# Softmax over 32,768 columns on one core: the first four stores in the load queue's order

## The chip, the core and the metric

The kernel runs on one core of one Trainium2 chip. The metric is device time in microseconds (us) of one execution, inputs and outputs in the chip's memory (HBM). The core's parts that matter here are VectorE (DVE), ScalarE (ACT), SyncE (SP), and the 16 DMA engines that carry data between HBM and on-chip memory (SBUF). A DMA is started by an instruction on SP or on ACT; each of the two has its own DMA queue, and the same 16 DMA engines serve both. In the profile SP's queue is q1 and ACT's is q10.

## The reference

A softmax with a temperature over the last axis of a 16 x 256 x 32768 array of float32:

```python
def reference(logits, temperature):            # temperature = 1.0
    scaled = logits / temperature
    scaled = scaled - scaled.max(axis=-1, keepdims=True)
    exp_scaled = np.exp(scaled)
    return (exp_scaled / exp_scaled.sum(axis=-1, keepdims=True)).astype(np.float32)
```

The input has 537 MB and so has the output; every byte is read once and written once.

## The kernel before

**Tiles.** The 4,096 rows are cut into halves, which gives 8,192 half rows of 16,384 elements. 128 of them, one for each SBUF partition, make a tile of 8.39 MB; there are 64 tiles, 0 to 63. A row's two halves lie on neighbouring partitions of one tile. SBUF holds three tiles at a time (`_BUFS = 3`); tile g lives in slot g mod 3, and its result is written over its input there.

**One tile's work** (class `Work`). The tile is cut into three column pieces of 6304, 5376 and 4704 (`_PLAIN`, line 11). DVE finds the negated maximum of each piece (line 188), ACT replaces each piece by its exponential with its own maximum and sums it (line 248), DVE swaps the two half rows' maxima and sums between partitions (206), takes the row's maximum (210), ACT makes the correction factors (259), and DVE forms the factor of each piece (217 to 233). Then the pieces are scaled: the first by ACT (267), the other two by DVE (239). The last two tiles use six smaller pieces (`_LATE`).

**Loads and stores.** `load(g)` (lines 119 to 131) is issued by SP. From tile 3 on it waits until the store of tile g - 3, which had the slot before, has landed. Load 3 is cut into two halves; each half waits for the matching half of store 0 only. `store(p, engine, ...)` (lines 133 to 146) waits until the pieces that it covers are scaled, and is then issued on the engine that it is given. Store 0 has two halves, store 61 four pieces, store 63 three.

**Who issues what, in which order.** An engine's instructions run in the order in which they are written, and a waiting instruction holds up all behind it on that engine. SP's program is: all loads 0 to 63 (lines 269 and 270), then the stores of tiles 62 and 63 (271 and 272), then a wait for everything (277 and 278). ACT's program is: tiles 0 to 3 written out, each followed by its store (289 to 291), a loop of 19 turns with three tiles and their stores in each (292 to 297), and tiles 61 to 63 written out, with the store of tile 61 (298 to 301). DVE's program has the same three parts and issues no DMA. The lines that set the order of the DMAs around the change are these:

```python
    for g in range(G):
        load(g)
    for g in range(G - _TAIL + 1, G):
        store(Place(g, G), nc.sync, None)
...
    for g in range(_HEAD):
        Work(Place(g, G)).scalar()
        store(Place(g, G), nc.scalar, None)
```

Here `G` is 64, `_HEAD` 4 and `_TAIL` 3. Text and code below name a load of tile g as Lg and a store as Sg, with a and b for halves.

Of the kernel before, what the change touches and what calls it, by code (L numbers as in the profile page):

```python
# [15 lines left out]
_TAIL = 3  # L16
# [48 lines left out]
def load_parts(g):  # L65
    if g == 3:
        return [(0, _W // 2), (_W // 2, _W // 2)]
    return [(0, _W)]


def store_parts(g, n):
    if g == 0:
        return [(0, _W // 2), (_W // 2, _W // 2)]
    if g == n - _TAIL:
        return list(_NEXT_STORES)
    return list(_LAST_STORES) if g == n - 1 else [(0, _W)]


def stored(g, n):
    first = [(("st", 0, g % _BUFS), 16 * (g // _BUFS + 1))]  # L80
    return first + [(("st", i, "of", g), 16) for i in range(1, n)]
# [3 lines left out]
def kernel(  # L85
# [6 lines left out]
    nc = tc.nc  # L92
# [12 lines left out]
    G = N * 2 // P  # L105
# [13 lines left out]
    def load(g):  # L119
        p = Place(g, G)  # L120
        rows = slice(g * P, (g + 1) * P)
        for j, (s, n) in enumerate(load_parts(g)):
            if g >= _BUFS:
                parts = store_parts(g - _BUFS, G)
                tokens = stored(g - _BUFS, len(parts))
                for (a, m), (which, value) in zip(parts, tokens):
                    if a < s + n and s < a + m:
                        nc.sync.wait_ge(sig[which], value)
            where = slice(p.slot * _W + s, p.slot * _W + s + n)
            key = ("ld", j, *p.key)  # L130
            sig.dma(key, nc.sync.dma_start(out=X[:, where], in_=x[rows, s : s + n]))

    def store(p, engine, first, some=slice(None)):
        g = p.g
        rows = slice(g * P, (g + 1) * P) if first is None else bass.ds(first, P)
        for i, (s, n) in list(enumerate(store_parts(g, G)))[some]:
            if p.looped:
                engine.wait_ge(sig[("scaled", *p.key)], p.n2)
            else:
                for group in (p.own, p.on_act):  # L140
                    for k in [k for k in group if k in p.over(s, n)][-1:]:
                        engine.wait_ge(sig[("scaled", k, *p.key)], p.n)
            where = slice(p.slot * _W + s, p.slot * _W + s + n)
            sig.dma(
                stored(g, len(store_parts(g, G)))[i][0], engine.dma_start(out=o[rows, s : s + n], in_=X[:, where])  # L145
            )
# [119 lines left out]
                xs = self.piece(k)  # L266
                self.scaled(a.mul(out=xs, in_=xs, mul=f[:, k : k + 1]), k, self.p.on_act)  # L267

    for g in range(G):
        load(g)  # L270
    for g in range(G - _TAIL + 1, G):
        store(Place(g, G), nc.sync, None)
    counts = {}
    for g in range(G):
        for which, value in stored(g, len(store_parts(g, G))):
# [12 lines left out]

    for g in range(_HEAD):
        Work(Place(g, G)).scalar()  # L290
        store(Place(g, G), nc.scalar, None)
    with nc.scalar.Fori(1, 1 + turns) as turn:
        turn2 = nc.scalar.snap(turn * 2)
        for j in range(_BUFS):
# [2 lines left out]
            store(p, nc.scalar, turn * (_BUFS * P) + (_HEAD + j - _BUFS) * P)  # L297
    for g in range(G - _TAIL, G):
        Work(Place(g, G)).scalar()
        if g == G - _TAIL:  # L300
            store(Place(g, G), nc.scalar, None)


# [33 lines left out]
```

## Time and profile before

| what | value |
|---|---|
| median of 3 runs (lowest to highest) | 2485.12 us (2484.16 to 2495.25) |
| profiled execution: its own time | 2484.74 us |
| profiled execution: span of its instructions | 2483.0 us |
| VectorE busy | 1526.2 us, 61% of the span |
| ScalarE busy | 1325.5 us, 53% |
| q1 (SP's DMA queue) | 553.65 MB, 51.6% of the 16 engines' time |
| q10 (ACT's DMA queue) | 520.10 MB, 48.4% |
| read from HBM and written to it | 536.87 MB each, 432 GB/s over the span |
| loads: issue to landing, shortest, median, longest | 22.0, 43.5, 64.4 us |

The span is what the profile's pages divide into; the execution's own time has 1.7 us more around it. The two queues' shares of the DMA engines' time add up to 100%. A DMA's time from issue to landing holds its waiting in the queue and the sharing of the DMA engines with the other queue, and so grows with what is in flight beside it.

### The profile page before, as it was taken

The numbers are of one execution on the slowest core, as the hardware profiler recorded it, in microseconds if no ns is written. First come the engines' busy times: TensorE is split into PE (matmuls) and PEld (weight loads), VectorE is DVE, ScalarE is ACT, GpSimd is POOL, SyncE is SP. The second block draws the span as 40 slices with busy tenths as digits, with TensorE's granted clock in tenths as the row PEclk, the third lists the DMA queues.
The fourth block names the chain that finished last, engine by engine and source line by source line (L and its number), as shares of the span: only waits on it lengthen the run. The fifth ranks groups of instructions, "written<-read, shape, count | busy, mean of one in ns | idle before, by whom it ended". The sixth has DMA issues, their size and how long they took to land.

```text
span 2483.0 us, 1810 instructions
## 1 busy us (share of the span) xinstructions
DVE 1526.2 (61%) x776; ACT 1325.5 (53%) x529; POOL 0.2 (0%) x4
## 2 busy tenths in 40 slices
DVE  5755665656656666566665665656656566565665
ACT  4644645546455464554654646546455464554655
POOL 0000000000000000000000000000000000000000
DMA  9999999999999999999999999999999999999999
GB/s 421 420 436 423 439 438 430 433 438 435 428 439 437 425 438 437 434 430 438 436 427 438 438 431 432 438 435 428 439 436 425 439 438 434 429 439 436 425 441 394
DMA packets 19443, 1073.78 MB, mean 432 GB/s; under 512 B 2160, under 2 KB 2160, under 8 KB 2160
## 3 DMA queue, kind: packets, MB, share of 16 engines
q1 hardware_dynamic: 9936, 553.65, 51.6%
q10 hardware_dynamic: 9504, 520.10, 48.4%
q14 instruction: 3, 0.02, 0.0%
HBM read 536.87 MB, written 536.87 MB: 432 GB/s over the span
## 4 chain that ended last, share of the span: by engine, by line
DMA 71%; DVE 22%; ACT 5%; issue 0%; ACTq 0%; DVEq 0%; SPq 0%
DMA xs<-in_logits_dram 36%; DMA out_dram<-xs 35%; DVE t L188 16%; DVE xs L239 5%; ACT xs L248 5%; ACT ee L259 0%; DVE junk L233 0%; DVE t L206 0%; DVE row L230 0%; DVE row L210 0%; DVE junk L217 0%; ACTq L145 0%; DVE row L217 0%; DVEq L204 0%; SPq L332 0%
## 5 line engine op out<-in xcount | busy, mean ns | idle before, releaser
L248 ACT ACTIVATE xs<-xs,t 128x6304 f32<-128x6304 f32 (+5 forms) x198 | 932.0, 4707 | 1052.2 <-DVE t L188 1045.3
L188 DVE TENSOR_REDUCE t<-xs 128x1 f32<-128x6304 f32 (+5 forms) x198 | 1110.1, 5663 | 616.9 <-DMA xs<-in_logits_dram 616.9
L267 ACT ACTIVATE xs<-xs,junk 128x6304 f32<-128x6304 f32 (+1 forms) x68 | 355.6, 5235 | 45.0 <-DVE junk L233 45.0
L239 DVE TENSOR_SCALAR xs<-xs,junk 128x5376 f32<-128x5376 f32 (+2 forms) x130 | 358.8, 2803 | 2.3
L206 DVE LOAD_MASK_SELECT t<-t x64 | 0.9, 14 | 282.8 <-ACT xs L248 282.8
L259 ACT ACTIVATE ee<-t,row 128x6 f32<-128x6 f32 (+1 forms) x64 | 19.2, 300 | 35.2 <-DVE row L210 35.2
L248 ACT ACTIVATION_READ_ACCUMULATOR xs<-xs,t 128x1 f32 x198 | 36.9, 186 | 0.0
L217 DVE CUSTOM_DVE_ANT_1 junk<-ee,t 128x6 f32<-128x6 f32 (+1 forms) x64 | 10.7, 167 | 23.5 <-ACT ee L259 23.5
L233 DVE TENSOR_SCALAR junk<-ee,row 128x3 f32<-128x3 f32 (+1 forms) x64 | 14.6, 229 | 2.3
L230 DVE RECIPROCAL row<-row 128x1 f32<-128x1 f32 x64 | 10.5, 163 | 2.2
L210 DVE TENSOR_REDUCE row<-t 128x1 f32<-128x6 f32 (+1 forms) x64 | 10.2, 159 | 2.2
L206 DVE STREAM_SHUFFLE t<-t 128x6 f32<-128x6 f32 (+1 forms) x64 | 10.4, 163 | 0.5
L217 DVE DVE_READ_ACCUMULATOR2_ANT row<- 128x1 f32 x64 | 5.3, 83 | 0.0
L248 ACT ACT_TABLE_LOAD x1 | 1.3, 1283 | 0.9 <-SPq L111 0.9
L318 POOL MEMSET const-bfloat16-1.0<- 128x1 bf16 x1 | 0.1, 102 | 0.0
L318 POOL MEMSET const-uint8-127<- 128x1 uint8 x1 | 0.1, 102 | 0.0
L318 POOL MEMSET const-float32-1.0<- 128x1 f32 x1 | 0.1, 99 | 0.0
L318 POOL MEMSET const-float32-0.0<- 128x1 f32 x1 | 0.1, 98 | 0.2 <-issue 0.2
## 6 DMA issues: line engine op xcount, KB each, us to landing
out_dram<-xs ACTq DMA_DIRECT2D x2, 4096.0 KB, 28.4
xs<-in_logits_dram SPq DMA_DIRECT2D x2, 4096.0 KB, 35.9
out_dram<-xs ACTq DMA_DIRECT2D x4, 2048.0 KB, 41.7
out_dram<-xs SPq DMA_DIRECT2D x2, 3072.0 KB, 18.7
out_dram<-xs SPq DMA_DIRECT2D x1, 2048.0 KB, 11.5
xs<-in_logits_dram SPq DMA_DIRECT2D x63, 43.5
out_dram<-xs ACTq DMA_DIRECT2D x60, 43.4
out_dram<-xs SPq DMA_DIRECT2D x1, 27.9
```

Of the source, the lines that this page charges most:

```text
L188: m = v.tensor_reduce(out=t[:, k : k + 1], in_=self.piece(k), axis=mybir.AxisListType.X, op=A.max, negate=True,)
L206: v.stream_shuffle(out=t[:, 2 * K : 4 * K], in_=t[:, 0 : 2 * K], mask=swap), "sh"
L210: v.tensor_reduce(out=r[:, 0:1], in_=tv[:, :, 0, :], axis=mybir.AxisListType.XY, op=A.min),
L217: v.tensor_tensor_reduce(out=f[:, 0 : 2 * K].rearrange("p (a k) -> p a k", a=2), in0=self.ev, in1=tv[:, :, 1, :], scale=1.0, scalar=0.0, o ...
L230: self.done(v.reciprocal(out=r[:, 2:3], in_=r[:, 1:2]), "rc")
L233: v.tensor_scalar_mul(out=f[:, 0:K], in0=e[:, 0:K], scalar1=r[:, 2:3]), "f"
L239: v.tensor_scalar_mul(out=xs, in0=xs, scalar1=f[:, k : k + 1]), k, self.p.own
L248: s = a.activation(out=xs, in_=xs, func=Exp, bias=t[:, k : k + 1], scale=inv_t, accum_out=t[:, K + k : K + k + 1],)
L259: a.activation(out=self.ev, in_=self.tv[:, :, 0, :], func=Exp, bias=r[:, 0:1], scale=-1.0),
L267: self.scaled(a.mul(out=xs, in_=xs, mul=f[:, k : k + 1]), k, self.p.on_act)
L318: nc = _bacc.Bacc("TRN2", target_bir_lowering=False, num_devices=1)
```

## The change

SP's program becomes one list, `order(n)`, in which the stores of tiles 0 to 3 stand between loads 0 to 4. ACT no longer issues a store that is in that list: it issues none behind tiles 0 to 3, the 57 of its loop (tiles 4 to 60) as before, and that of tile 61 as before. The stores of tiles 62 and 63 stay on SP behind the last load. All waits of each load and store stay the same, and so do their sizes.

```diff
+def order(n):
+    plan = [("L", 0), ("L", 1), ("L", 2), ("S", 0), ("L", 3), ("S", 1), ("S", 2)]
+    plan += [("L", 4), ("S", 3)] + [("L", g) for g in range(5, n)]
+    return plan + [("S", n - 2), ("S", n - 1)]
...
-    for g in range(G):
-        load(g)
-    for g in range(G - _TAIL + 1, G):
-        store(Place(g, G), nc.sync, None)
+    for what, g in order(G):
+        if what == "L":
+            load(g)
+        else:
+            store(Place(g, G), nc.sync, None)
...
     for g in range(_HEAD):
         Work(Place(g, G)).scalar()
-        store(Place(g, G), nc.scalar, None)
+        if ("S", g) not in order(G):
+            store(Place(g, G), nc.scalar, None)
...
     for g in range(G - _TAIL, G):
         Work(Place(g, G)).scalar()
-        if g == G - _TAIL:
+        if ("S", g) not in order(G):
             store(Place(g, G), nc.scalar, None)
```

With its halves, SP's list begins L0, L1, L2, S0a, S0b, L3a, L3b, S1, S2, L4, S3, L5, L6 and so on.

## The prediction

> **What bounds the kernel now.** I read the page's engine shares first: DVE is busy 61% of the span and ACT 53%, so neither is the bound over the whole. Next the page's lines on DMA:
>
> ```profile
> DMA  9999999999999999999999999999999999999999
> HBM read 536.87 MB, written 536.87 MB: 432 GB/s over the span
> ```
>
> The DMA engines are busy in every one of 40 slices. The question is then how far the DMA rate falls below its best, and where; the view by stretches, at edges that I chose by the phases of the pipeline, tells (columns: stretch, length, DVE, ACT, POOL busy, PE clock, DMA share, GB/s):
>
> ```profile
> 0.00:52.00 52.00, 24.11 (x13) 21.95 (x9) 0.20 (x4) 1.00 0.99 423
> 52.00:140.00 88.00, 62.57 (x27) 49.95 (x19) 0.00 (x0) 1.00 1.00 424
> 140.00:232.00 92.00, 56.10 (x34) 53.37 (x22) 0.00 (x0) 1.00 1.01 431
> 232.00:348.00 116.00, 71.02 (x36) 61.55 (x24) 0.00 (x0) 1.00 1.00 434
> 464.00:2322.00 1858.00, 1144.99 (x577) 992.54 (x385) 0.00 (x0) 1.00 1.00 434
> 2404.00:2483.00 79.00, 48.37 (x32) 43.05 (x32) 0.00 (x0) 1.00 0.95 409
> ```
>
> From 232 us on the rate is 434 GB/s, turn after turn, with no gap. 1073.74 MB at 434 GB/s take 2474.1 us; the span is 2483.0. All that any reordering could win is the difference of 8.9 us (0.36%), and only part of it lies where this change works.
>
> Last, the chain of waits in order of time (columns: start, length, what) shows the loop's rhythm:
>
> ```profile
> 580.75 43.45 DMA out_dram<-xs
> 624.22 43.47 DMA xs<-in_logits_dram
> 667.72 17.35 DVE t L188 x3
> ...
> 690.96 5.61 DVE xs L239 x2
> 696.73 43.33 DMA out_dram<-xs
> ```
>
> A slot's round is store 43.5, load 43.5, compute and issue 29.0, together 696.73 - 580.75 = 115.98 us for three tiles in three slots, 38.66 a tile. The two transfers of one tile at 434 GB/s need 2 x 8.389 MB / 434 = 38.66 us. So the chain looks as if it alternated between load, compute and store, but its period is just the DMA engines' work. One transfer that shares the engines half and half takes 38.7 us; each takes 4.8 us more, because it queues behind its forerunner. These 2 x 4.8 = 9.6 us in each round are slack: a slot may come late by that much before an engine runs dry. "DMA-bound" is therefore what has to be tested: **does the new order ever leave the DMA engines without work, or make them slower?**
>
> **The change part by part.** The comparison of the two programs by engine shows the five DMAs of stores 0 to 3 gone from ACT and standing in SP's list where the diff puts them; nothing else moves. Five issues at 0.34 us (the duration of the store issues on ACT in the timeline) leave ACT, which sits idle 1052.2 us before line 248 waiting for DVE: worth nothing. They add five issues of 0.33 to 0.42 us to SP, which does nothing but wait and issue: cost nothing as long as the queue has work, which I now check. What ACT's waits for scaling held up was only ACT's own next exponential, and that waits for DVE's maximum anyway.
>
> Units: one tile is 19.3 us of the 16 engines (8.389 MB / 434 GB/s). The first loads confirm it with a single queue at work: by the issue view of narrow windows, L0 is issued at 0.94 and lands 22.0 later (22.9), L1 at 1.38 and lands 40.9 later (42.3), 19.4 behind. The 22.0 of L0 hold 2.7 us of start. Compute of a tile that is not waiting for data takes 28.6 us (in the chain, DVE starts at 23.00, 51.72, 80.33, and scales tile 2 until 108.96), so S0 is ready at 51.8, S1 at 80.4, S2 at 109.0, as now. Then the new order, one queue, first in first out:
>
> - L2 behind L1: 42.3 to 61.6. Before, S0 shared the engines from 51.8, and L2 landed at 1.84 + 64.4 = 66.2.
> - S0a, S0b issued at 51.8 and 52.2: they run 61.6 to 71.3 to 80.9. (Before: S0a landed at 51.8 + 20.6 = 72.4, S0b at 88.4.)
> - L3a waits for S0a (71.3), runs behind S0b, 80.9 to 90.6; L3b waits for S0b (80.9), runs to 100.2. (Before: 101.5 and 131.2.)
> - S1, ready at 80.4, is held on SP behind L3b's wait until about 81.4; runs 100.2 to 119.5.
> - S2 issued at 109.0, runs 119.5 to 138.9. L4 waits for S1 (119.5), runs 138.9 to 158.2 (before: landed at 165.9).
> - S3: tile 3's data are all there at 100.2, DVE is free at 109.0, so it is ready at 137.6; runs 158.2 to 177.5. (Before: issued at 153.4, as L3b landed late.)
> - L5 waits for S2 (138.9) and stands behind S3's wait (137.6), which is over by then; runs from 177.5. L6 waits for S3 (177.5).
> - S4 on ACT's queue from 158.2 + 29.0 = 187.2; from here the two queues share as before.
>
> At each of these issues the queue still holds work in front: 9.8 us at 51.8, 9.6 at L3a, 9.7 at L3b, 10.5 at S2, 19.4 at L4, 20.6 at S3, 38.6 at L5, and L5's own 19.3 at L6. The least is 9.6, against 2.7 from issue to data. No gap opens, and no load is held behind a store that becomes ready later than the load's own condition. So what SP's order brings forward (tile 3 by 15.8 us, tile 4 by 8) is order among bytes, not fewer bytes: the engines were carrying something else in that time, and must still carry it.
>
> Terms of the sum:
>
> - **The head's rate.** 52 to 140 and 140 to 232 run at 424 and 431: 88 x (1 - 424/434) + 92 x (1 - 431/434) = 2.0 + 0.6 = 2.7 us below the loop's rate. The new order may win all of it, or nothing. Against it stands a cost that before doesn't show, one queue going from loads to stores and back at full depth. Its rows: the worst 10 us of this head, 50 to 60, where the first store starts, moved 367 GB/s, 10 x (1 - 367/434) = 1.5 us lost; SP's queue in the new order has six such turns (L2/S0, S0/L3, L3/S1, S2/L4, L4/S3, S3/L5), at most 9.3 us. The other bound is the tail, where q1 passes from L63 to S62 and S63: 2404 to 2464 ran at 433, nothing lost. The tail's row is the same situation, so I take it: turns at about 0, and a third of the 2.7 won, -0.9.
> - **The loop.** Its phase can come out differently, but its rate is at 434 both ways: 0.
> - **The tail.** It starts when L62 lands, 2404.6. DVE then works back to back to the end of scaling at 2458.8 (54.2 us), and the last two pieces, 6.3 MB, need 14.5 us and 2.7 of start: 71.4. The engines owe 2481.5 - 2404.6 = 76.9 us (at 2481.5 SP's final wait is over, by the view of line 131). The engines' debt is the longer by 5.5. If the loop's 9.6 us of slack lay otherwise, so that L62 came 9.6 later against the same bytes, the end would move by 9.6 - 5.5 = 4.1. Nothing in the change sets that: each load still waits for its slot's store, which pulls the phase to the same round. I take 0, bound +4.1.
>
> Sum: 2484.7 (the profiled execution's own time, 0.4 below the median of 2485.1) - 0.9 = **2484 us**, own range 2481 to 2487.
>
> A rule of the Trainium skill speaks against the change ("DMA: Bandwidth & Descriptors", section "Anatomy of one DMA"): each DMA has a fixed part of about 2.0 us for setup and completion, which does not shrink with size (fitted there for DMAs issued by GpSimd). If a single queue showed it at every DMA, the ten from S0a to L6 would add some 20 us by that figure, as an estimate. The trace of before does not bear that out for a queue with work waiting: L1 landed 19.4 us behind L0, its bare transfer.
>
> **The rivals.**
>
> *The waits show in one queue (slower).* With loads and stores in one line there is no second queue to fill a pause. If each of the nine dependent issues (S0a, L3a, L3b, S1, S2, L4, S3, L5, L6) emptied the queue and paid L0's 2.7 us of start, the loss is 24 us: 2509. It decides where the work in front of an issue falls under 2.7 us; for that some wait must come 7 us later than I have it. For it: S1 does stand behind L3b's wait. Against it: 9.6 us at the tightest place. Chance 0.06.
>
> *Turns cost (about the same or a little slower).* The 1.5 us at each of six turns: 2484.7 + 9.3 = 2494. For it the 367 GB/s at 50 to 60; against it the tail's 433. Chance 0.08.
>
> *The phase moves the tail.* +4.1: 2489. For it: the head enters the loop with tile 4 about 8 us earlier. Against it: before's own head is irregular too (load waits of 15.7, 12.5 and 8.4 us on DVE) and has settled by 232. Chance 0.08.
>
> *Faster by over 0.5%* would be under 2472, less than the bytes take at the best rate of any long stretch: 0.01. That the change does nothing of what it says is excluded by the order of instructions.
>
> **How the numbers follow.** The forecast of 2484 has 0.77. Half a per cent, 12.4 us, is about what a measurement of this kernel tells from no change; the three runs before already spread over 11 us. Inside 2472.3 to 2497.1 lie the forecast, the turns and the phase: same 0.93; slower 0.06; faster 0.01. The range reaches down to 2480 (2.7 won in the head, and 2 of the 79 x (1 - 409/434) = 4.6 us lost in the tail) and up to the 2494 of the turns; outside remain the waits and the faster case, 0.07.
>
> **What would show it.** Right: by the issue view five stores of tiles 0 to 3 on SP's queue, L3b landing near 100 and S3 issued near 138, about 433 GB/s over 60 to 190, ACT's first store near 187, a round of 116 us and 434 GB/s from 232 on, and 2404 to the end as before. Wrong: a stretch of the head well under 424 (turns), or a DMA share that drops between 52 and 180 with SP waiting for scaling (waits), or the tail's rate below 409 (phase). My forecast falls if one queue alone cannot keep the 16 engines full when its loads and stores alternate.

## The result: 0.34% slower, outside the range

The changed kernel takes 2497.18 us (median of 17 runs, 2491.87 to 2507.81), before takes 2486.7 (17 runs, 2484.16 to 2498.93). The ratio is 1.0034, 95% interval 1.0021 to 1.0048: slower by some 8.5 us, a third of a per cent, where 2484 was forecast, with a range of 2481 to 2487 for the sum and of 2480 to 2494 with the rivals inside it. Every run on record counts as undisturbed (fast), and the ratios here and below are the record's own and not quotients of the medians, which lie 10.5 us apart in this case (the means 8.6). The profiled execution of the changed kernel took 2493.68 us, with a span of 2491.9, 8.9 more than before.

The page's lines on DMA look as before, and show only that the engines are still called busy throughout:

```profile
DMA  9999999999999999999999999999999999999999
HBM read 536.87 MB, written 536.87 MB: 431 GB/s over the span
```

The view by stretches of the changed kernel, at the edges used for before (stretch, length, DVE, ACT, POOL busy, clock, DMA share, GB/s), tells where the time went:

```profile
0.00:52.00 52.00, 23.96 (x13) 21.95 (x9) 0.20 (x4) 1.00 0.99 423
52.00:140.00 88.00, 71.04 (x36) 62.00 (x24) 0.00 (x0) 1.00 1.00 428
140.00:232.00 92.00, 43.00 (x23) 36.71 (x16) 0.00 (x0) 1.00 1.00 430
232.00:348.00 116.00, 69.69 (x29) 60.12 (x22) 0.00 (x0) 1.00 1.00 423
348.00:464.00 116.00, 71.51 (x36) 62.07 (x25) 0.00 (x0) 1.00 0.99 420
464.00:2322.00 1858.00, 1144.58 (x579) 992.50 (x387) 0.00 (x0) 1.00 1.00 433
```

Of before, the stretch 348 to 464, for comparison:

```profile
348.00:464.00 116.00, 71.33 (x37) 61.81 (x25) 0.00 (x0) 1.00 1.00 434
```

The stretch whose order was changed, 52 to 232, is no slower than before (428 and 430 here, 424 and 431 before). Below before's 434 are the stretches **behind** it: 232 to 348 by 116 x 11/434 = 2.9 us, 348 to 464 by 3.7, and the loop, where the bytes of the packets give 433.4 GB/s after 434.1, by 2.7. L62 lands at 2413.9 in place of 2404.6, 9.3 late, and from there to the end it takes 78.0 us, as before (78.4). So nothing is lost in the tail.

Closer, around the place where stores pass from SP's queue to ACT's:

```profile
190.00:236.00 46.00, 23.80 (x13) 20.63 (x9) 0.00 (x0) 1.00 1.00 425
236.00:242.00 6.00, 0.67 (x1) 0.62 (x1) 0.00 (x0) 1.00 1.05 350
242.00:348.00 106.00, 65.02 (x27) 55.50 (x21) 0.00 (x0) 1.00 1.01 432
348.00:360.00 12.00, 6.50 (x9) 6.49 (x4) 0.00 (x0) 1.00 0.88 377
360.00:370.00 10.00, 6.14 (x1) 0.00 (x0) 0.00 (x0) 1.00 0.91 328
```

Three dips: 350 GB/s at 236 to 242, 377 and 328 at 348 to 370. Stretches as short as these hold only two to five packets of each engine, and a packet counts where it begins, so their rates alone say little. The trace's records of single DMA packets say of what kind the dips are. In the loop a packet of 64 KB (one partition's row of a tile) takes 2418 ns on its DMA engine, load or store alike. Summed over all packets and divided by 16 engines, time above that pace was 5.2 us before and 11.8 after; time in which an engine had no packet grew by 2.6. 6.6 + 2.6 = 9.2 us, which is the difference between the ends of the last packets (2481.1 and 2490.3). **Longer packets make up most of it, dry engines the rest.** By place, the long packets of 64 KB cost 1.5 us at 236 to 242, 1.7 at 348 to 370 (with 1.8 of dry engines), and 2.6 spread over the loop from 464 on, where before has 0.15.

And the records of landings show how the 16 engines come apart. A DMA has landed when the last of its 16 parts has. Before, the first and last part of a DMA lie 0.7 us apart at the start and at most 6.0 in the loop. In the changed kernel it is 8.6 for L6 (236.5 to 245.1), 11.3 for L7, 14.5 for S6 (305.8 to 320.2). A slot's next transfer waits for the slowest engine; a round has 9.6 us of slack; at 350 to 358 the fast engines have run out of work, since S8 and L10 are issued only at 356.0 and 358.8.

What began it? The two DMAs at the first dip, by the issue view of narrow windows (us from issue to landing; L7 issued at 234.79, S5 at 236.85):

```profile
xs<-in_logits_dram SPq DMA_DIRECT2D x1, 49.0
```

```profile
out_dram<-xs ACTq DMA_DIRECT2D x1, 46.3
```

L7 waits for S4, which lands at 234.8. S5 waits for tile 5, which landed at 207.8, since L5 had stood behind S3 in SP's queue. So both queues get their next transfer within 2.1 us of each other, just as L6 ends on most engines (236.5). Before, the corresponding issues were S5 at 232.2 and L7 at 237.5, 5.4 apart. Nearness of issue alone is not enough, though: before has S4 and L6 issued 1.0 us apart (194.9 and 195.9), and its long packets there, 194 to 220, cost 0.8 us. And the packets of the two do not begin at once: L7's first start at 236.2 to 237.1 on 13 engines, and it is the 16 load packets that start next, at 238.6 to 240.2, L7's second on most engines, that take 3.1 to 4.2 us; S5's first packets start only at 242.3.

### The profile page after: what moved, and what is told of

Its sections match the earlier page's. It is cut to its first block, busy times and chain, and to the rows that moved or that the text cites. A ratio compares the mean times of both kernels' runs of the same rounds, so it can differ in the third digit from the quotient of the medians.

```text
span 2491.9 us, 1810 instructions
## 1 busy us (share of the span) xinstructions
DVE 1526.0 (61%) x776; ACT 1325.5 (53%) x529; POOL 0.2 (0%) x4
## 4 chain that ended last, share of the span: by engine, by line
DMA 72%; DVE 21%; ACT 5%; another core or an unknown queue 1%; issue 0%; ACTq 0%; SPq 0%; DVEq 0%
DMA out_dram<-xs 36%; DMA xs<-in_logits_dram 36%; DVE t L194 15%; DVE xs L245 5%; ACT xs L254 5%; ACT ee L265 0%; ACT xs L273 0%; DVE junk L239 0%; DVE t L212 0%; DVE row L236 0%; DVE row L216 0%; DVE junk L223 0%; ACTq L151 0%; DVEq L210 0%
## 5 line engine op out<-in xcount | busy, mean ns | idle before, releaser
L236 DVE RECIPROCAL row<-row 128x1 f32<-128x1 f32 x64 | 10.5, 163 | 2.2
```

What stands on the lines that cost most here:

```text
L236: self.done(v.reciprocal(out=r[:, 2:3], in_=r[:, 1:2]), "rc")
```

## The experiments

Two readings were possible at first. *Handover*: the stream of stores breaks off where the stores change queues. *Turns*: loads and stores in one queue cost at each passage, as the prediction's rival had it. A third, *any shift*, says that every change of the head's phases costs this much.

### First four: which part of the order carries the loss

**e1_s0_only**: only store 0 stays in SP's list.

```diff
-    plan = [("L", 0), ("L", 1), ("L", 2), ("S", 0), ("L", 3), ("S", 1), ("S", 2)]
-    plan += [("L", 4), ("S", 3)] + [("L", g) for g in range(5, n)]
+    plan = [("L", 0), ("L", 1), ("L", 2), ("S", 0)] + [("L", g) for g in range(3, n)]
```

> Only store 0 stands in SP's list (L0 L1 L2 S0 L3 ...); stores 1 to 3 are back on ACT. Theory of the handover (the loss arises where the stores pass from SP's queue to ACT's and the stream of stores breaks off shortly before the loop, here between S3 landing and S4's data, 232 to 240 us in the changed kernel): S1 is ready at 80.4, before S0b lands near 82, so the stream does not break at the handover, and the loss is at most 2 us against before. Rival, turns in one queue (8.9 us for six passages between loads and stores, 1.5 each): two passages, +3 us. Rival, any shift of the head's phases costs as much as this change: +6 to +10 us.

Measured: 2488.03 against 2487.46, ratio 0.9993 (0.9977 to 1.0009). No loss. (The profiled execution, with a span of 2514.3, is the one of 13 that lies apart; the other twelve took 2485.8 to 2493.8. In it the engines came apart: L5's parts land over 14.2 us, S4's over 19.8, and packets took 33.9 us above their pace, where before has 5.2. S3 was issued there at 161.4, as L4 ended, 158.9 to 163.5, and L5 began. So one program can lose or not lose from one execution to the next; no trace of the twelve is kept.)

**e2_s3_back**: stores 0 to 2 in SP's list, store 3 on ACT.

```diff
-    plan += [("L", 4), ("S", 3)] + [("L", g) for g in range(5, n)]
+    plan += [("L", g) for g in range(4, n)]
```

> Stores 0 to 2 stand in SP's list, store 3 is back on ACT and shares the engines with L4. Handover theory: S4 then becomes ready some 25 us after S3 has landed, with loads alone in between, a longer break than in the changed kernel: a loss of 6 to 10 us, with load landings of the 16 engines spread over more than 8 us between 200 and 350. Turns in one queue: four passages, +6 us, and it lies before 180. Any shift: +6 to +10.

Measured: 2501.65, ratio 1.0049 (1.0029 to 1.007), worse than the whole change. But not at the place that any theory named. Its stretches:

```profile
140.00:190.00 50.00, 0.00 (x0) 0.00 (x0) 0.00 (x0) 1.00 0.96 354
190.00:220.00 30.00, 24.59 (x13) 20.67 (x8) 0.00 (x0) 1.00 1.01 439
220.00:240.00 20.00, 16.50 (x3) 13.98 (x5) 0.00 (x0) 1.00 0.98 423
240.00:250.00 10.00, 8.49 (x10) 6.69 (x4) 0.00 (x0) 1.00 0.63 270
250.00:260.00 10.00, 10.00 (x2) 5.33 (x1) 0.00 (x0) 1.00 0.93 315
260.00:348.00 88.00, 50.99 (x26) 44.62 (x19) 0.00 (x0) 1.00 1.00 433
```

In 140 to 190 the engines had work nearly all the time, L4 in one queue and S3 in the other, and moved 354 GB/s: 50 x (1 - 354/434) = 9.2 us lost. Of these the long packets are 7.3 us, engines without a packet 1.3. S2 ends at 139.3 to 140.0; L4's first packets start behind it, and those of S3, issued at 137.3, start at 141.7 to 142.5, one packet later on each engine. Then, at 190 to 220, stores are missing for 30 us and loads alone run at 439; the break costs nothing, and neither does S4's joining in at 221. The dip at 240 to 260 is a dry queue (4.5 us) and another pair begun together (S5 issued at 248.5, L7 at 249.2; 2.1 us of long packets). That pair's trouble is over by 260, and its parts land less than 1 us apart.

**e3_l5_first**: load 5 ahead of store 3.

```diff
-    plan += [("L", 4), ("S", 3)] + [("L", g) for g in range(5, n)]
+    plan += [("L", 4), ("L", 5), ("S", 3)] + [("L", g) for g in range(6, n)]
```

> The changed kernel with L5 put ahead of S3 in SP's list. Tile 5 lands near 180 in place of 207.8, S5 is ready near 210, while S3 and S4 still run: the stream of stores doesn't break at the handover. Handover theory: +0 to +4 us against before. Turns in one queue: six passages as before, +9 us. Any shift: +6 to +10.

Measured: 2485.14 against 2487.46, ratio 0.9989 (0.9976 to 1.0003). The loss is gone, with as many passages in one queue as in the changed kernel. Its stretch 267 to 281 has loads alone (S5 landed at 267.1, S6 was issued at 278.9), and the stores come back into a running load without a dip:

```profile
267.00:281.00 14.00, 8.99 (x11) 10.30 (x6) 0.00 (x0) 1.00 1.02 440
281.00:348.00 67.00, 45.29 (x24) 41.33 (x16) 0.00 (x0) 1.00 1.01 437
```

**e4_one_queue**: all stores in SP's list, none on ACT.

```diff
-    plan = [("L", 0), ("L", 1), ("L", 2), ("S", 0), ("L", 3), ("S", 1), ("S", 2)]
-    plan += [("L", 4), ("S", 3)] + [("L", g) for g in range(5, n)]
-    return plan + [("S", n - 2), ("S", n - 1)]
+    plan = [("L", 0), ("L", 1), ("L", 2), ("S", 0), ("S", 1), ("L", 3)]
+    for g in range(2, n - 3):
+        plan += [("S", g), ("L", g + 2)]
+    return plan + [("L", n - 1), ("S", n - 3), ("S", n - 2), ("S", n - 1)]
...
-            store(p, nc.scalar, turn * (_BUFS * P) + (_HEAD + j - _BUFS) * P)
```

> All 64 stores stand in SP's list, each between two loads (S g, L g+2), and ACT issues none: one queue for everything, no sharing between queues, no handover. Handover theory: no loss in the loop; 434 GB/s from 140 us to the end and within 4 us of before, either way. Turns in one queue: 120 passages at 1.5 us, +180 us. Any shift: +6 to +10.

Measured: 2497.5, ratio 1.0043 (1.0017 to 1.0068), but in two groups: six runs at 2487.8 to 2489.6 and six at 2505.5 to 2510.5. The profiled execution, span 2486.6, is of the first:

```profile
232.00:348.00 116.00, 71.52 (x36) 61.99 (x24) 0.00 (x0) 1.00 1.00 433
1000.00:2322.00 1322.00, 817.09 (x417) 708.46 (x274) 0.00 (x0) 1.00 1.00 434
```

Some 120 passages between loads and stores in one queue, at 434 GB/s: **turns cost next to nothing**. The span is 3.6 us above before's, at most 0.03 us for each passage where 1.5 was the rival's price. The six quick runs are within the 4 us expected, the median is not; what the second group loses, no trace here shows.

So turns are out (e3, e4), and any shift is out (e1, e3). The handover in its first form falls too: breaks in the stream of stores of 14 and 30 us cost nothing in e3 and e2. What the dips have in common is a load and a store that begin close together. The new theory, *common start*: **a load and a store that begin on both queues at the same moment lengthen each other's packets and drive the 16 engines apart**; the rest follows from the late landings.

### Four more: the common start, moved

For these a tile's scaling was delayed by one more reduction on VectorE, after the exponentials:

```diff
             self.wait(v, "sum")
+            if self.p.g == 3 and not self.p.looped:
+                base = self.p.slot * _W
+                v.tensor_reduce(
+                    out=r[:, 3:4], in_=X[:, base : base + 8192], axis=mybir.AxisListType.X, op=A.max
+                )
```

**e5_s3_later**: e2_s3_back with these lines.

> The run with store 3 back on ACT, in which L4 (SP's queue) and S3 (ACT's queue) began within 2 us of each other at 140 and the stretch 140 to 190 moved 354 GB/s; here VectorE does one more reduction of 8192 columns in tile 3 (about 8.7 us, its result is not used), so S3 begins near 148, in the middle of L4. Theory of the common start (a load and a store that begin together on engines with nothing else to do lengthen each other's packets until they fall out of step): 140 to 190 at 425 GB/s or more, and at least 7 of the 13 us above before go. Rival, engines in lockstep (all 16 do the same at the same moment after the stretch with one queue): still below 390 GB/s. Rival, the break in the stream of stores: S4 comes no earlier, so the loss stays at 10 us or more.

Measured: 2486.38, ratio 0.9981 (0.9967 to 0.9995) against before. Adding 8.7 us of work took away all of e2's 0.49%. Its stretches, to be held against e2's:

```profile
140.00:190.00 50.00, 23.33 (x8) 18.33 (x6) 0.00 (x0) 1.00 0.98 422
190.00:240.00 50.00, 33.78 (x22) 28.55 (x12) 0.00 (x0) 1.00 1.01 437
```

422 in place of 354 (425 had been expected; some 430 over both stretches, since a window counts a packet where it begins). L4 lands near 170 in place of 190. The engines had been in lockstep in both runs when S3 came (S2's parts landed within 0.5 and 0.8 us), so lockstep alone is not the cause. The break in the stream of stores is not tested here, since S4 did come earlier (199.4, in e2 219.4); against it stands the 439 GB/s of e2's own break.

**e6_head7**, the control: the changed kernel with

```diff
-_HEAD = 4
+_HEAD = 7
```

> The changed kernel with tiles 4 to 6 written out ahead of the loop in place of its first turn (_HEAD = 7), nothing else: a control for the next two. All theories: as the changed kernel, +7 to +10 us against before.

Measured: 2497.84, ratio 1.0028 (1.0014 to 1.0042): as the change. In its profile L7 is issued at 233.5 and S5 at 235.4, and the parts of L7 land 13.5 us apart, those of S6 24.4:

```profile
236.00:242.00 6.00, 3.24 (x1) 0.00 (x0) 0.00 (x0) 1.00 1.04 426
242.00:348.00 106.00, 61.77 (x27) 51.86 (x21) 0.00 (x0) 1.00 1.00 406
```

The loss is there, but not the 350 GB/s at 236 to 242 of the changed kernel.

**e7_s5_later**: the control with the reduction in tile 5, over 4096 columns:

```diff
+            if self.p.g == 5 and not self.p.looped:
...
+                    out=r[:, 3:4], in_=X[:, base : base + 4096], axis=mybir.AxisListType.X, op=A.max
```

> The control with seven tiles written out, and one more reduction of 4096 columns (about 4.4 us, result not used) on VectorE in tile 5: S5 is issued near 241 in place of 237, and L7 has begun alone at 237. Theory of the common start: the long packets of 236 to 242 go (350 GB/s there in the changed kernel), and the loss falls to 4 us or less. Rival, the break in the stream of stores: it is longer by 4 us, so the loss stays or grows, 8 to 12 us. Rival, any shift of the head: 6 to 10 us.

Measured: 2487.26, ratio 0.9981 (0.9966 to 0.9995). L7 is issued at 232.8 and S5 at 239.9; L7's parts land 1.6 us apart, S6's 3.8. Against the control it is the second stretch that tells, 431 in place of 406:

```profile
236.00:242.00 6.00, 6.00 (x3) 3.81 (x1) 0.00 (x0) 1.00 1.01 437
242.00:348.00 106.00, 68.69 (x36) 61.46 (x24) 0.00 (x0) 1.00 1.00 431
```

In 236 to 300 the packets of 64 KB take 5.3 us above their pace in the control, and less than 0.1 here. The two programs differ in the one reduction alone, and what it moves first is S5's issue (239.9, in the control 235.4): so it is S5's start beside L7 that sets this loss off.

**e8_s4_halves**: the control with store 4 in two halves (in `store_parts`):

```diff
-    if g == 0:
+    if g in (0, 4):
         return [(0, _W // 2), (_W // 2, _W // 2)]
```

> The control with seven tiles written out, and store 4 in two halves of 8192 columns, so the first store on ACT's queue comes in packets of half the size and L5 beside it gets the larger share of the engines: L5 lands near 200 in place of 207.8, S5 is ready near 229, before S4 has landed. Theory of the common start: no pair of load and store begins together near 237, loss 3 us or less. Break in the stream of stores: the break closes, loss 3 us or less as well. Any shift of the head: 6 to 10 us.

Measured: 2486.56, ratio 0.9982 (0.9968 to 0.9995). S5 is issued at 231.8, L7 at 238.2, and no dip follows. This one adds no work. It is faster than the changed kernel, and level with before or a little better: 0.18% by the ratio, 0.06% by the medians (2488.12 for before), and its quickest run, 2484.53, is not below before's, 2483.97. Common start and break in the stream expected the same of it, so it does not separate these two.

### The last four: how far apart is enough

The edit of e5_s3_later with fewer columns, and e2_s3_back with store 3 in halves:

```diff
-base + 8192      # e5_s3_later
+base + 1024      # e9_later_1us
+base + 2048      # e10_later_2us
+base + 4096      # e11_later_4us
```

```diff
-    if g == 0:
+    if g in (0, 3):   # e12_s3_halves
         return [(0, _W // 2), (_W // 2, _W // 2)]
```

**e9_later_1us**

> Dose of the shift, smallest: as the run with S3 later, but with a reduction of only 1024 columns (about 1.1 us), so S3 begins about 140.5, within L4's first packets. Common start with a window of about 2 us: still slow, 140 to 190 below 400 GB/s, +8 to +13 us against before. If one packet's time (2.4 us) isn't the measure and any shift helps: +3 us or less.

**e10_later_2us**

> Dose of the shift: 2048 columns (about 2.2 us), S3 begins about 141.7, still within one packet of L4's start. Common start with a window of about one packet: between the two, 360 to 420 GB/s in 140 to 190, +4 to +10 us. If any shift helps: +3 us or less.

**e11_later_4us**

> Dose of the shift: 4096 columns (about 4.4 us), S3 begins about 144, two packets behind L4. Common start: 140 to 190 at 415 GB/s or more, +3 us or less against before. If only a shift as large as 8.7 us helps (half a tile, since then the backlog behind L4 changes too): +8 us or more.

**e12_s3_halves**

> The run with store 3 back on ACT, and store 3 in two halves of 8192 columns; it begins with L4 as there, but its packets have half the size. Common start whatever the packets: 140 to 190 below 390 GB/s, +8 us or more. If the trouble needs load and store packets of the same size in step: 415 GB/s or more, and since L4 then has the larger share and lands near 178, +3 us or less.

| run | S3 issued at | GB/s, 140 to 190 | L4's parts land apart by | median, us | ratio to before (95%) |
|---|---|---|---|---|---|
| e2_s3_back | 137.3 | 354 | 7.0 | 2501.65 | 1.0049 (1.0029 to 1.007) |
| e9_later_1us | 138.6 | 405 | 11.4 | 2498.61 | 1.0021 (1.0003 to 1.0039) |
| e10_later_2us | 139.8 | 421 | 0.7 | 2489.06 | 1.0002 (0.9992 to 1.0013) |
| e11_later_4us | 141.8 | 418 | 2.4 | 2486.65 | 0.9991 (0.9983 to 1.0) |
| e5_s3_later | 146.1 | 422 | 1.8 | 2486.38 | 0.9981 (0.9967 to 0.9995) |
| e12_s3_halves | 137.4 | 421 | 3.4 | 2491.45 | 1.0015 (1.0005 to 1.0026) |

The records of single packets show when the two begin. S2 ends, and L4's first packets start, at 139 to 140 in all of them. S3's first packets start 3.5 to 5.1 us after its issue: in e2 behind one packet of L4 on every engine (141.7 to 142.5), in e9 behind one on three engines (142.1 to 142.3) and behind two on thirteen (144.2 to 145.0), in e10 behind two on all (144.2 to 145.0), in e11 behind three, in e5 behind five. What the packets of 64 KB took above their pace in 140 to 190 is 7.3, 1.8, 0.3, 0.4 and 0.4 us in these five. **With two packets of L4 ahead of S3 on every engine, the trouble is gone here.** The two profiles at that step:

```profile
140.00:190.00 50.00, 2.54 (x1) 0.00 (x0) 0.00 (x0) 1.00 0.97 405
190.00:240.00 50.00, 39.98 (x23) 36.31 (x16) 0.00 (x0) 1.00 0.94 408
240.00:260.00 20.00, 20.00 (x5) 13.27 (x4) 0.00 (x0) 1.00 0.74 279
260.00:348.00 88.00, 49.99 (x25) 43.73 (x19) 0.00 (x0) 1.00 1.01 434
```

for a shift of 1.1 us, and for 2.2:

```profile
140.00:190.00 50.00, 13.24 (x3) 6.46 (x3) 0.00 (x0) 1.00 0.98 421
190.00:240.00 50.00, 39.98 (x23) 34.86 (x14) 0.00 (x0) 1.00 1.02 438
240.00:260.00 20.00, 14.99 (x11) 17.59 (x8) 0.00 (x0) 1.00 1.00 410
```

In S3's issue 1.2 us decide between them: with the shorter shift the last part of L4 lands at 187.4, tile 4 is late, and at 215 to 260 the engines are without packets for 8.3 us; with the longer one L4 lands whole at 176.7. e9's 405 GB/s is a little more than the 400 expected; ten of its twelve runs took 2497 to 2503 us, but by the ratio it lost 5 us and not 8 to 13. e10 did better than the 360 to 420 GB/s and +4 to +10 us expected of it: S3 began at 144.2, not at the 141.7 expected, and so behind two packets and not within the first.

In e12 half-size packets beside full-size ones keep the pace (421), although they too begin behind one packet of L4, on 14 engines. So the size of the packets mattered there; one run does not show more. Its remaining +0.15%, 3.7 us where 3 or less was expected (interval 1.2 to 6.5), lies elsewhere:

```profile
190.00:240.00 50.00, 30.35 (x21) 29.16 (x12) 0.00 (x0) 1.00 0.96 397
260.00:348.00 88.00, 51.52 (x33) 48.81 (x22) 0.00 (x0) 1.00 1.01 434
```

S4 (issued at 200.0) and L6 (200.7) both come after S3 and L5 have landed at about 200: the queues are dry for 3.1 us, and then long packets cost 2.0.

This is a third pair begun together, beside S5 and L7 in e2 (issued at 248.5 and 249.2) and in e9 (245.6 and 246.1), and the three **limit the theory**. All had full-size packets, were issued within 0.8 us of each other and found the queues dry or nearly so. Each cost 1.9 to 2.1 us of long packets, within some 10 us of the start, and then 433 to 434 GB/s were back and the two DMAs' parts landed at most 1.6 us apart. So a common start lengthened packets in all of them, but it drove the engines apart in none of them.

## Why the prediction was wrong

**What held.** DMA is the bound, from end to end. The head's schedule held until its last line: L3b landed at 102.5 (100.2 forecast), S3 was issued at 137.7 (137.6), L4 landed at 161.8 (158.2), S4 was issued on ACT at 190.8 (187.2). No queue ran dry up to there. The head's rate rose as forecast: 2.0 + 0.6 us lost against the loop's pace became 88 x 6/434 + 92 x 4/434 = 1.2 + 0.8, so 0.6 won where 0.9 was taken. *Turns cost* is refuted by e3 and e4, *the waits show in one queue* by the same rates; *the phase moves the tail* did not happen either (78.0 us after 78.4). So none of the three slower rivals names the loss that came. The rule of the Trainium skill ("DMA: Bandwidth & Descriptors", section "Anatomy of one DMA") on a fixed part of every DMA did not show with work waiting in the queue. From S0b's landing at 82.6 to S3's at 181.2, six DMAs with the bytes of five tiles took 98.5 us, 1.9 over the 96.6 of the bare transfers; the rule's 2.0 us at each of the six would be 12 us, as an estimate.

**The step that failed** is "from here the two queues share as before", and with it the term of the loop, "its rate is at 434 both ways: 0". I had worked out the schedule up to S4's issue and stopped one round too early. Carried on with the same numbers, and some 1.5 us from issue to data (L0's packets start 1.0 to 2.4 us after its issue): S4 begins at 188.7 and, sharing, ends 38.7 later, at 227.4. L5 had 8.1 of its 19.3 us left and ends at 204.9. L6 shares until 227.4 and runs alone to 235.5, where L7 begins behind it. S5, ready 29.0 after L5, is issued at 233.9 and begins at 235.4. So on paper a load and a store begin on both queues at once (measured: issues at 234.8 and 236.9); I would have seen the coincidence, if not its price. What it cost is what the term of 0 had to hold: 2.9 us in 232 to 348, 3.7 in 348 to 464 and 2.7 in the loop behind. The price was in no row of before that I used: two queues at work were 434 GB/s in every long stretch. The only hint, the 367 GB/s of 50 to 60 where the first store joins the loads, I priced at 1.5 us as a passage in one queue. By the packets it is 0.8 us; and in the changed kernel L2's packets are long by 1.2 us at 55 to 60, with one queue at work and S0 issued but still waiting. So what that row prices is not shown.

**The second mistake** is in the slack. 9.6 us a round was taken as a reserve against a late slot. It is also, as I read it, what the 16 engines may drift apart before the fastest run dry, and in before's loop up to 6.0 us of it are already in use for that. Dry engines are the smaller part of the loss, 2.6 of 9.2 us. The range covered a moved tail (+4.1), and not a loop that loses in its first rounds.

**What stays open.** That the loss is set off by S5 starting beside L7 is shown by e7 against e6, and the like for S3 beside L4 by e2, e9, e10, e11 and e5. Why packets lengthen then is not shown; in the changed kernel the first long ones are L7's, before S5's first packet starts. Nor is it shown why the engines came apart after some of these starts (L7 in e6: 13.5 us) and not after others (1.6 at most in the three pairs from dry queues). The spread of the landings (11.4 us in e9, 0.7 in e10) would fit engines that take load and store in a different order from one another, as e9's three engines do, but no record here names a packet's engine. In the changed kernel most engines had two packets of L7 ahead of S5, which sufficed in e10; there L6's parts landed over 8.6 us, so "the same moment" is not one moment for all engines. And e4's slower group was not caught in a profile.

## What to carry to other kernels

With two DMA queues that fill the engines, look not only at whether a queue ever holds nothing, but at whether a load and a store of equal packets begin on both close together, as here just after a stretch with one queue at work. Here a store issued 2.4 to 8.8 us later, or a first store cut in halves, took all or most of the loss away. Work the schedule out until it repeats, not until the change ends. A landing is that of the slowest engine: compare the first part's landing with the last, and hold the difference against the slack of the round.

## What the runs showed of the hardware

- A load and a store in packets of 64 KB, the store's first packet one packet behind the load's on each engine, moved 354 GB/s in 140 to 190 of e2_s3_back; with the store issued 2.4 to 8.8 us later the same two moved 418 to 422 (e10, e11, e5), and loads alone 439 (e2, 190 to 220).
- Three pairs of a load and a store issued within 0.8 us of each other on dry or nearly dry queues cost 1.9 to 2.1 us of long packets each, and no more (e2 and e9 near 250, e12 near 200).
- One queue with loads and stores in alternation holds 434 GB/s (e4_one_queue, 1000 to 2322), as two queues do (before).
- The parts of one DMA landed up to 24.4 us apart over the 16 engines (S6 of e6_head7).
- Adding 4.4 us of VectorE work to one tile made a kernel of some 2,500 us faster by 10.6 us (medians of e7_s5_later and its control).
